# Up-projection of an encoder block: the places of two plain matmuls, of the product copies and of the pair sums are fixed in the instruction order

## The chip, the cores and the metric

The kernel runs on one core of one Trainium2 chip. The metric is the device time of one execution in microseconds (us). The engines are TensorE (PE; its weight loads are a row of their own, PEld), VectorE (DVE), ScalarE (ACT), GpSimd (POOL) and SyncE (SP), which here only issues DMAs.

## The reference

One layer of a streaming encoder on 512 tokens of width 1024: attention, then a gated feed-forward block with a causal convolution of width 3. The change lies in the second part:

```python
def conv_glu(x, w_up, conv_w, conv_b, w_down):
    hid = x @ w_up
    hid = lax.conv_general_dilated(
        hid, conv_w[:, None, :], window_strides=(1,),
        padding=((CONV_WIDTH - 1, 0),),
        dimension_numbers=('NWC', 'WIO', 'NWC'),
        feature_group_count=2 * D_FF) + conv_b
    gate, up = hid[..., :D_FF], hid[..., D_FF:]
    return (jax.nn.silu(gate) * up) @ w_down
...
        x = x + mixed @ w_out[l]
        x = x + conv_glu(rms_norm(x, norm2_g[l]), w_ffn_up[l], ffn_conv_w[l],
                         ffn_conv_b[l], w_ffn_down[l])
```

With D_FF = 2816, the up-projection makes 22 chunks of 128 gate columns and 128 up columns each.

## The kernel before, in words

**Numbers in two halves.** Every operand of a matmul is cut into a high part (a cast to fp32r on ACT) and a low part (the rest, a subtraction on DVE), and each product is three matmuls: high by high, high by low, low by high. `hth` and `htl` are the two halves of the normed activations, transposed, for all 512 tokens; `whi`/`wlo`, `w2h`/`w2l` and `wxh`/`wxl` are halves of weights. The cut of the weights of chunk j + 1 runs while chunk j is multiplied (`run_chunk`, which takes one step of `split_gen` per step of the chunk's body).

**Plain chunks.** Chunks 2, 3, 6, 9, 12, 15, 19 and 21 multiply directly (`up_body`, `up_mm`): 8 steps of the contraction, three matmuls each, for the gate (`pg`) and for the up columns (`pu`), all 512 tokens wide: 48 matmuls. Chunks 0 and 1 do the same in two halves of 256 tokens.

**Seven-product chunks.** The twelve chunks in `SEVEN` (`up_seven`) use seven products of half-size blocks in place of eight. A product is 4 contraction steps by three matmuls, 256 wide, so a chunk is 84 matmuls. There are four banks, `b1`, `b5`, `b7` and `b6`. The first three hold a first product, are copied out to `pc` by ACT (L1177, L1181, L1185), and then a second product is accumulated on top of the first one: the second half of a bank can't begin before its copy. `ts` are sums of token blocks, made once (`token_sums`). From chunk 11 on (`SUMS`) the sums of weight blocks are cut on the chip as well, which adds two casts and two subtractions to the chunk ahead (`split_seven`, L242 and L243).

**Held matmuls.** Where a plain chunk comes ahead of a seven-product one (3, 6, 9, 12, 15 and 19), `up_mm` keeps back the last two matmuls of `pu`: the last three are at L1000, L1001 and L1002, and the latter two are written down behind the first three matmuls of the next chunk's first product (`late["end"]`).

**Behind a chunk.** The gate is convolved and passed through silu (`gate`: ACT L990 and L1014, DVE L992 and L993), so are the up columns, and the two are multiplied (DVE L1089). After every second chunk `pair_sums` makes sums of blocks for the down-projection, which are cut into halves: by DVE (L1053) or, for pairs 1 to 8, by a negated copy on ACT (L1061) and an accumulating DMA of GpSimd (L1062).

**What sets the order.** No one writes the order of an engine by hand. A scheduler places the instructions when the program is built, from the sequence of the source, from priorities (`tc.high_priority`), and from an internal model of when operands are ready. It may therefore put matmuls of a later chunk ahead of matmuls that wait for a copy, and it may take the held matmuls in either order with those of the next chunk. `behind(ins, others)` adds an edge of order alone: the instruction stands after the others, with no semaphore for it.

Of the kernel before, what the change touches and what calls it, by code (L numbers as in the profile page):

```python
# [74 lines left out]
def block_kernel(ctx: ExitStack, tc: tile.TileContext, x, xt, params, g2, rbx, wts, wd0, wd1, out):  # L75
# [28 lines left out]
    G.memset(nhalf, -0.5)  # L104
    qg8 = pool_c.tile([P, 1], F32, tag="qg8", name="qg8")

    def rstd_of(ss, n, width, name):

        r = pool_c.tile([P, 8], F32, tag="rs", name=name, bufs=4)
        V.tensor_scalar(r[:, :n], ss, 1.0 / width, EPS, op0=ALU.mult, op1=ALU.add)  # L110
        G.tensor_tensor(r[:, :n], r[:, :n], nhalf[:, :n], op=ALU.pow)
        return r
# [3 lines left out]
    order = [key for key, _, _ in CHUNKS]  # L116

    pos = {k: i for i, k in enumerate(order)}
    raws, splits, extras, late = {}, {}, {}, {"halves": (), "casts": (), "products": ()}
    FIRST_DN = order.index("dn0_0")  # L120
    keep = {}

# [110 lines left out]
    def split_seven(i, raw, hi, lo):  # L233

        wh, wl = extras.pop(i - pos["up0"])
        splits[order[i]] = tuple(t.rearrange("p (k c) -> p k c", c=P) for t in (hi, lo, wh, wl))
        parts = [(hi, lo, raw, slice(0, 1024)), (hi, lo, raw, slice(1024, 2048))]
        if i - pos["up0"] in SUMS:
            parts[1:1] = [(wh, wl, wl.bitcast(F32), slice(0, 1024))]
            parts += [(wh, wl, wl.bitcast(F32), slice(1024, 1536))]  # L240
        for n, (h, l, src, sl) in enumerate(parts):
            A.copy(h[:, sl], src[:, sl])  # L242
            V.tensor_tensor(l[:, sl], src[:, sl], h[:, sl].bitcast(F32), op=ALU.subtract)  # L243
            if n < len(parts) - 1:
                yield

    def split_gen(i, pieces):

        if i >= len(order):
            return  # L250
        key = order[i]
        kn = CHUNKS[i][1]
        raw = raws.pop(i)
        if is_seven(i) and i - pos["up0"] not in extras:
            fetch_extra(i - pos["up0"])
        sh = 48 if key[:2] in ("qA", "kA", "vB") else 16 if key in ("up0", "up1") or is_seven(i) else 0
        n = 512 * kn if i >= FIRST_DN else 2048
        hi = wp.tile([P, 2112], F32R, tag="whi", name=f"whi_{key}")[:, sh:sh + n]
        lo = wp.tile([P, 2112], F32R, tag="wlo", name=f"wlo_{key}")[:, sh:sh + n]
        splits[key] = (hi.rearrange("p (k c) -> p k c", k=kn), lo.rearrange("p (k c) -> p k c", k=kn))  # L260
        if i >= FIRST_DN:
            yield from split_down(i - FIRST_DN, raw, hi, lo)
        elif is_seven(i):
            yield from split_seven(i, raw, hi, lo)
        n = 2048 // pieces
        cuts = CUTS[0] if i == 0 else [n * j for j in range(pieces + 1)] if i < FIRST_DN and not is_seven(i) else ()
        for j, sl in enumerate(map(slice, cuts, cuts[1:])):
            if i == 0 and j == 0:
                V.tensor_copy(hi[:, sl], raw[:, sl])
            else:  # L270
                A.copy(hi[:, sl], raw[:, sl])  # L271
                if i == 0 and j == 1:
                    yield
                    V.tensor_tensor(lo[:, 0:256], raw[:, 0:256], hi[:, 0:256].bitcast(F32), op=ALU.subtract)
            if (i, j) != (0, 0):
                V.tensor_tensor(lo[:, sl], raw[:, sl], hi[:, sl].bitcast(F32), op=ALU.subtract)  # L276
                if j < len(cuts) - 2:
                    yield


        nxt = {0: None, 1: i + 3, 2: None}.get(i - FIRST_DN, i + 2)
        if nxt is not None and nxt < len(order):
            next(load(nxt))
        j = i + 1 - pos["up0"]
        if j in SEVEN and all(k < j - 2 for k in SEVEN if k < j and (k in SECOND) == (j in SECOND)):
            fetch_extra(j)
        yield
# [433 lines left out]

    a_exps, b_sigs = [], []

    def behind(ins, others):

        for o in others:
            tc.add_manual_dep(ins.ins, o.ins.name, mybir.DependencyInfo(
                mybir.DependencyClass.NoSync, mybir.DependencyReason.DATA), reason="table order")
        return ins

    def soft_b(h, t, ps):


# [261 lines left out]
    def up_mm(ps, hi, lo, o, c0, c1, held=None):  # L995

        for k in range(NK):
            if held is not None and k == NK - 1:
                sh, sl, mh, ml = hi[:, k, o:o + P], lo[:, k, o:o + P], hth[:, k, c0:c1], htl[:, k, c0:c1]
                PE.matmul(ps[:, c0:c1], sh, mh, start=False, stop=False)  # L1000
                held.append(lambda: PE.matmul(ps[:, c0:c1], sh, ml, start=False, stop=False))  # L1001
                held.append(lambda: PE.matmul(ps[:, c0:c1], sl, mh, start=False, stop=True))  # L1002
                yield
# [13 lines left out]
    def pair_sums(i):  # L1017
# [38 lines left out]
        def by_dma():  # L1056

            for a, o, src in ((ay, 256, t["s42"]), (ax, 768, t["st"][:, 0:256]), (ay, 0, u[:, 768:1024]),
                              (ax, 0, u[:, 0:768])):
                n, sl = a.shape[-1] // 2, slice(o, o + src.shape[-1])  # L1060
                A.activation(a[:, n + o:n + sl.stop], src, AF.Copy, scale=-1.0)  # L1061
                G.dma_start(a[:, n + o:n + sl.stop].bitcast(F32), src, accum_op=ALU.add)  # L1062
                A.copy(a[:, sl], src)
        if 0 < i < 9:
# [19 lines left out]
    def up_fin(j, pg, pu, g=None):  # L1084
# [4 lines left out]
        late["fin"] = (V.tensor_tensor(u, g, u, op=ALU.mult),)  # L1089
        if j % 2 == 1 and j // 2 < 9:  # L1090
            steps = pair_sums(j // 2)
            for step in steps:
                step()
            if j // 2 < 7:
                G.dma_start(ayd[j // 2], pairs[j // 2][1].bitcast(F32))

    def up_body(j):
        def body(hi, lo):
# [7 lines left out]

            def end():
                for mm in held or ():
                    mm()
                up_fin(j, pg, pu, g)  # L1110
            if held:
                late["end"] = end
            else:
                end()
            if j in (2, 3):
                next(late["ts"])
        return body
# [39 lines left out]
    def up_seven(j):  # L1157
        def body(hi, lo, wh, wl):
# [6 lines left out]
            def prod(ps, w, b, h, first=True, last=True):  # L1165
                for k in range(4):
                    sh, sl = w[0][:, 4 * b + k, :], w[1][:, 4 * b + k, :]
                    for n, (st, mv) in enumerate(((sh, h[0]), (sh, h[1]), (sl, h[0]))):
                        PE.matmul(ps, st, mv[:, k, :], start=first and k == 0 and n == 0,  # L1169
                                  stop=last and k == 3 and n == 2, skip_group_check=True)  # L1170
                    if late.get("end"):
                        late.pop("end")()
            r, w = (hi, lo), (wh, wl)
            B = lambda a, q: [t[:, 4 * a:4 * a + 4, q] for t in (hth, htl)]
            prod(b1, r, 0, B(0, left), last=False)
            with tc.high_priority(60):
                A.copy(pc[:, 0], b1)  # L1177
            yield
            prod(b5, w, 0, ts[1], last=False)
            with tc.high_priority(60):  # L1180
                A.copy(pc[:, 1], b5)  # L1181
            yield
            prod(b7, r, 1, ts[3], last=False)
            with tc.high_priority(60):
                A.copy(pc[:, 2], b7)  # L1185
            V.tensor_tensor(pc[:, 1], pc[:, 1], pc[:, 2], op=ALU.add)
            yield
            prod(b6, w, 1, ts[2])
            V.tensor_tensor(hu[:, right], b6, pc[:, 0], op=ALU.add)
            yield  # L1190
            prod(b1, r, 2, B(1, left), first=False)
            A.copy(hg[:, left], b1)
            yield
            prod(b5, w, 2, B(1, right), first=False)
            V.tensor_tensor(hg[:, right], b5, hu[:, right], op=ALU.add)
            g = gate(j, hg)
            yield
            prod(b7, r, 3, ts[4], first=False)
            V.tensor_tensor(hu[:, left], b7, hu[:, right], op=ALU.add)
            V.tensor_tensor(hu[:, right], hu[:, right], pc[:, 1], op=ALU.add)  # L1200
            up_fin(j, None, hu, g)
            yield
        return body
# [232 lines left out]
```

## Time and profile before

| | |
|---|---|
| median of 3 runs | 717.42 us (717.33 to 717.8) |
| profiled execution | 718.12 us |
| its span, first to last instruction | 716.4 us |
| TensorE clock granted, mean | 0.999 |
| PE, PEld, DVE, ACT busy in 395 to 607 us | 211.24, 195.71, 180.77, 144.20 us of 212.00 |
| the same in 607 to 716 us | 105.04, 86.23, 90.17, 46.92 us of 109.00 |

The up-projection lies between 395 and 607 us, the down-projection behind it. Matmuls are pipelined: a row's length is that of one matmul from its first read to its modelled end, longer than the distance from one start to the next, and the distance is what counts for throughput. The chain of waits merges neighbours of one line into pieces with a count, so a long piece's length over its count is that distance.

### The profile page before, as it was taken

Reading aid. Unit: us, or ns where it says so; the run is one execution under the profiler, and the core shown is the slowest. Engines: PE = TensorE matmul, PEld = TensorE weight load, DVE = VectorE, ACT = ScalarE, POOL = GpSimd, SP = SyncE. Lnnn points to the kernel's source line nnn. Section 1 sums busy time; section 2 is a strip of 40 time slices with the busy share of each in tenths; the row PEclk is TensorE's granted clock in tenths of the full one; section 3 lists DMA queues with packets and bytes.
Section 4 is the critical chain, followed back from the end, with each engine's and each line's share of the span. In section 5 each row is a group of like instructions: output and inputs, shape, how many; then the busy total and the mean of one; then the engine's idle time right before and its main releaser. Section 6 shows DMA issues by size and latency. Waiting matters only on the chain.

```text
span 716.4 us, 11264 instructions
## 1 busy us (share of the span) xinstructions
PE 709.9 (99%) x4091; PEld 623.6 (87%) x4091; DVE 589.0 (82%) x1049; ACT 432.2 (60%) x803; POOL 85.7 (12%) x123
## 2 busy tenths in 40 slices
PE   9999999999999999999999999999999999999997
PEld 7889998888988888888889889999999998888885
DVE  6668878786999999769475698888788979998686
ACT  6576656667876777434245557668667874544531
POOL 2501200000121211000003002212012111000000
PEclk9999999999999999999999999999999999999999
DMA  9722235444434473685957949999788889674563
GB/s 316 284 82 89 86 121 190 178 162 175 164 130 150 147 280 127 214 305 196 378 198 286 306 172 328 310 359 244 222 213 246 254 232 376 213 245 172 180 206 117
DMA packets 51863, 154.97 MB, mean 216 GB/s; under 512 B 5600, under 2 KB 12384, under 8 KB 44000
## 3 DMA queue, kind: packets, MB, share of 16 engines
q1 hardware_dynamic: 44256, 133.67, 52.9%
q0 software_dynamic: 7264, 20.45, 10.8%
q8 instruction: 32, 0.52, 0.3%
q14 instruction: 23, 0.19, 0.1%
q10 hardware_dynamic: 288, 0.14, 0.1%
HBM read 116.49 MB, written 30.41 MB: 205 GB/s over the span
## 4 chain that ended last, share of the span: by engine, by line
PE 92%; DVE 3%; DMA 3%; SPq 1%; ACT 0%; issue 0%; POOL 0%; DVEq 0%
PE p L1169 16%; PE P L1269 15%; PE vA L433 3%; PE uA L433 3%; PE gB L300 2%; PE gB L301 2%; PE qkB L302 2%; PE gB L302 2%; PE qkB L300 2%; PE qkB L301 2%; PE wo L300 2%; PE wo L301 2%; PE wo L302 2%; PE gA L300 2%; PE pg L300 2%; PE pg L301 2%
## 5 line engine op out<-in xcount | busy, mean ns | idle before, releaser
L165 ACT CAST whi_dn<-raw_dn 128x1024 fp32r<-128x1024 f32 x33 | 34.4, 1052 | 26.5 <-PE P L1269 18.7
L1269 PE MATMUL P<-whi_dn,ax 128*128 128x512 f32 x144 | 44.4, 389 | 0.0
L161 DVE TENSOR_TENSOR wlo_dn<-raw_dn,whi_dn 128x1024 fp32r<-128x1024 f32 x33 | 40.1, 1222 | 5.3 <-ACT whi_dn L165 5.3
L1269 PE MATMUL P<-whi_dn,ay 128*128 128x512 f32 x132 | 40.8, 389 | 0.0
L744 POOL TENSOR_SCALAR_AFFINE_SELECT bB<-bB 128x128 f32<-128x128 f32 x32 | 21.8, 686 | 143.7 <-DVE bB L743 135.1
L1169 PE MATMUL p<-ts,whi_up 128*128 128x256 f32 x192 | 35.5, 279 | 0.0
L301 PE MATMUL pg<-htl,whi_up 128*128 128x512 f32 (+1 forms) x96 | 34.0, 354 | 0.0
L302 PE MATMUL pg<-hth,wlo_up 128*128 128x512 f32 (+1 forms) x96 | 34.0, 354 | 0.0
L300 PE MATMUL pg<-hth,whi_up 128*128 128x512 f32 (+1 forms) x96 | 33.9, 353 | 0.0
L207 DVE TENSOR_TENSOR pkr<-pkr 128x512 f32<-128x512 f32 x40 | 27.4, 686 | 7.0 <-DMA pkr<-in_wts 4.1
L1269 PEld LDWEIGHTS P<-whi_dn,ax 128*128 128x128 f32 x144 | 27.0, 188 | 5.6
L301 PE MATMUL pu<-htl,whi_up 128*128 128x512 f32 (+1 forms) x90 | 31.5, 351 | 0.0
L300 PE MATMUL pu<-hth,whi_up 128*128 128x512 f32 (+1 forms) x90 | 31.5, 350 | 0.0
L302 PE MATMUL pu<-hth,wlo_up 128*128 128x512 f32 (+1 forms) x90 | 31.5, 349 | 0.0
L243 DVE TENSOR_TENSOR wlo_up<-raw_up,whi_up 128x1024 fp32r<-128x1024 f32 x24 | 28.8, 1219 | 1.7 <-ACT whi_up L242 1.7
L1169 PEld LDWEIGHTS p<-ts,whi_up 128*128 128x128 f32 x192 | 29.6, 189 | 0.1
L1269 PEld LDWEIGHTS P<-whi_dn,ay 128*128 128x128 f32 x132 | 24.8, 188 | 5.1
L1269 PE MATMUL P<-wlo_dn,ax 128*128 128x512 f32 x72 | 28.0, 389 | 0.0
L742 DVE TENSOR_TENSOR_SCAN aB<-aB,reset 128x127 f32<-128x127 f32 (+3 forms) x32 | 25.9, 816 | 2.6 <-ACT aB L737 2.5
L1169 PE MATMUL p<-ts,wlo_up 128*128 128x256 f32 x96 | 26.9, 280 | 0.8 <-DVE wlo_up L243 0.8
L276 DVE TENSOR_TENSOR wlo_up<-raw_up,whi_up 128x1024 fp32r<-128x1024 f32 (+1 forms) x26 | 24.6, 973 | 2.9 <-ACT whi_up L271 2.8
L1169 PE MATMUL p<-hth,whi_up 128*128 128x256 f32 x96 | 26.8, 279 | 0.0
(350 smaller groups left out, 2539.2 us busy)
## 6 DMA issues: line engine op xcount, KB each, us to landing
parked<-pkr SPq DMA_DIRECT2D x45, 256.0 KB, 2.8
raw_dn<-in_wd SPq DMA_DIRECT2D x11, 1024.0 KB, 4.9
pkr<-in_wts SPq DMA_DIRECT2D x10, 1024.0 KB, 6.8
raw_up<-in_wts SPq DMA_DIRECT2D x10, 1024.0 KB, 5.3
raw_up<-in_wts SPq DMA_DIRECT2D x12, 512.0 KB, 6.1
raw_dn<-in_wd SPq DMA_DIRECT2D x11, 512.0 KB, 3.5
wxl_up<-parked SPq DMA_DIRECT2D x21, 256.0 KB, 5.7
ayd<-ay POOLq DMA_DIRECT2D x7, 768.0 KB, 6.8
```

The lines of the kernel that those rows point to most:

```text
L161: chain("halves", V.tensor_tensor(o, x, y, op=op))
L165: chain("casts", A.copy(hi[:, sl], src))
L207: V.tensor_tensor(b[o], b[x], b[y], op=op)
L243: V.tensor_tensor(l[:, sl], src[:, sl], h[:, sl].bitcast(F32), op=ALU.subtract)
L276: V.tensor_tensor(lo[:, sl], raw[:, sl], hi[:, sl].bitcast(F32), op=ALU.subtract)
L300: ins = PE.matmul(ps, sh, mh, start=first, stop=False)
L301: PE.matmul(ps, sh, ml, start=False, stop=False)
L302: PE.matmul(ps, sl, mh, start=False, stop=last)
L433: PE.matmul(pss[t], st[:, 4 * half + k, t * P:(t + 1) * P], mv[:, k, :], start=half == 0 and k == 0 and j == 0, stop=half == 1 and k == 3 ...
L742: V.tensor_tensor_scan(ar, ar, reset[:, S - n:S - 1][:, ::-1], 1.0, op0=ALU.mult, op1=ALU.max)
L1169: PE.matmul(ps, st, mv[:, k, :], start=first and k == 0 and n == 0, stop=last and k == 3 and n == 2, skip_group_check=True)
L1269: chain("products", PE.matmul(dst, st, mv, start=first and n == 0, stop=last and n == 2, skip_group_check=True))
```

## The change

Five edits, all in the up-projection; the amount of arithmetic is the same.

1. *The held pair.* The last matmul of a plain chunk that is not kept back (`late["pre"]`) stands ahead of the next chunk's first three, these ahead of the two held ones, and every further matmul of seven-product chunks is put behind the last of the pair (`late["flip"]`). Each edge is of order alone.
2. *The casts of weights.* Each cast of `split_seven` and `split_gen` is put behind the copy of a product that was written last (`late["pcs"]`), so the casts of the next chunk's later parts follow the copies of `b1`, `b5` and `b7`.
3. *The pair sums.* Only the first step stays in `up_fin`; the rest is kept in `owed` and paid in a later chunk, after the third copy (with the negated copies behind it, `late["copied"]`) or at the end of chunk 2, 6 or 12. Pair 8 is paid at once.
4. *The sums of `hu`.* The left half takes the fourth product and the right half is derived from it; four additions as before.
5. `behind` stands further up in the file.

```diff
         for n, (h, l, src, sl) in enumerate(parts):
-            A.copy(h[:, sl], src[:, sl])
+            behind(A.copy(h[:, sl], src[:, sl]), late["pcs"])
...
-                A.copy(hi[:, sl], raw[:, sl])
+                behind(A.copy(hi[:, sl], raw[:, sl]), late["pcs"])
...
-                PE.matmul(ps[:, c0:c1], sh, mh, start=False, stop=False)
+                late["pre"] = (PE.matmul(ps[:, c0:c1], sh, mh, start=False, stop=False),)
...
-                A.activation(a[:, n + o:n + sl.stop], src, AF.Copy, scale=-1.0)
+                behind(A.activation(a[:, n + o:n + sl.stop], src, AF.Copy, scale=-1.0), late["copied"])
...
             steps = pair_sums(j // 2)
-            for step in steps:
-                step()
-            if j // 2 < 7:
-                G.dma_start(ayd[j // 2], pairs[j // 2][1].bitcast(F32))
+            steps[0]()
+
+            def rest_(i=j // 2):
+                for step in steps[1:]:
+                    step()
+                if i < 7:
+                    G.dma_start(ayd[i], pairs[i][1].bitcast(F32))
+            owed.append(rest_)
+            if j == 17:
+                owed.pop()()
...
                 for mm in held or ():
-                    mm()
+                    late["flip"] = (behind(mm(), late["flip"]),)
                 up_fin(j, pg, pu, g)
...
+            if j % 2 == 0:
+                pay()
...
-                        PE.matmul(ps, st, mv[:, k, :], start=first and k == 0 and n == 0,
-                                  stop=last and k == 3 and n == 2, skip_group_check=True)
+                        mm = PE.matmul(ps, st, mv[:, k, :], start=first and k == 0 and n == 0,
+                                       stop=last and k == 3 and n == 2, skip_group_check=True)
+                        behind(mm, late["pre" if late.get("end") else "flip"])
                     if late.get("end"):
+                        late["flip"] = (mm,)
                         late.pop("end")()
...
             with tc.high_priority(60):
-                A.copy(pc[:, 0], b1)
+                late["pcs"] = (A.copy(pc[:, 0], b1),)
...
+            if j % 2 == (j - j % 2 in SEVEN and j - j % 2 + 1 in SEVEN):
+                late["copied"] = (third,)
+                pay()
             prod(b6, w, 1, ts[2])
-            V.tensor_tensor(hu[:, right], b6, pc[:, 0], op=ALU.add)
+            V.tensor_tensor(hu[:, left], b6, pc[:, 0], op=ALU.add)
+            V.tensor_tensor(hu[:, right], hu[:, left], pc[:, 1], op=ALU.add)
...
-            V.tensor_tensor(hg[:, right], b5, hu[:, right], op=ALU.add)
+            V.tensor_tensor(hg[:, right], b5, hu[:, left], op=ALU.add)
...
-            V.tensor_tensor(hu[:, left], b7, hu[:, right], op=ALU.add)
-            V.tensor_tensor(hu[:, right], hu[:, right], pc[:, 1], op=ALU.add)
+            V.tensor_tensor(hu[:, left], b7, hu[:, left], op=ALU.add)
```

The order of PE where plain chunk 12 gives way to chunk 13, before. `pu12` is the bank of the up columns of chunk 12, `p1_13` and `p5_13` are the banks `b1` and `b5` of chunk 13:

```order
L302 MATMUL pu12_5571<-hth_102,wlo_up12_5447 128x512
L1000 MATMUL pu12_5571<-hth_102,whi_up12_5446 128x512
L1001 MATMUL pu12_5571<-htl_103,whi_up12_5446 128x512
L1002 MATMUL pu12_5571<-hth_102,wlo_up12_5447 128x512
L1169 MATMUL p5_13_5641<-ts1_4467,wxh_up13_5469 128x256 x2
L1169 MATMUL p1_13_5640<-hth_102,whi_up13_5584 128x256
L1169 MATMUL p1_13_5640<-htl_103,whi_up13_5584 128x256
L1169 MATMUL p5_13_5641<-ts1_4467,wxl_up13_5470 128x256
```

The same place now:

```order
L309 MATMUL pu12_5558<-hth_102,wlo_up12_5434 128x512
L1000 MATMUL pu12_5558<-hth_102,whi_up12_5433 128x512
L1185 MATMUL p1_13_5640<-hth_102,whi_up13_5571 128x256
L1185 MATMUL p1_13_5640<-htl_103,whi_up13_5571 128x256
L1185 MATMUL p1_13_5640<-hth_102,wlo_up13_5572 128x256
L1001 MATMUL pu12_5558<-htl_103,whi_up12_5433 128x512
L1002 MATMUL pu12_5558<-hth_102,wlo_up12_5434 128x512
```

Three 256-wide matmuls of the first product now stand between L1000 and the two held ones. Before, this was so ahead of chunks 4, 7 and 10; now it is ahead of 4, 7, 10, 13, 16 and 20.

The order of ACT while chunk 4 is multiplied, before. `ub` and `cg` belong to the convolutions of chunks 2 and 3, `ax0` and `ay0` to the sums of pair 0, `pc4` are the copies of the products of chunk 4:

```order
L1052 CAST ax0_4402<-ub_4147 128x768
L242 CAST whi_up5_4622<-raw_up5_4450 128x1024 x2
L990 ACTIVATE ub_4147<-pu3_4502,par_91 128x512
L1014 ACTIVATE cg2_4462<-cg2_4462 128x512
L1177 COPY pc4_4580<-p1_4_4576 128x256
L1052 CAST ay0_4403<-st0_4404 128x512
L1181 COPY pc4_4580<-p5_4_4577 128x256
L1185 COPY pc4_4580<-p7_4_4578 128x256
L990 ACTIVATE cg3_4543<-pg3_4501,par_91 128x512
```

And now:

```order
L1052 CAST ax0_4402<-ub_4147 128x768
L990 ACTIVATE ub_4147<-pu3_4502,par_91 128x512
L1014 ACTIVATE cg2_4453<-cg2_4453 128x512
L1195 COPY pc4_4580<-p1_4_4576 128x256
L1052 CAST ay0_4403<-st0_4404 128x512
L249 CAST whi_up5_4609<-raw_up5_4441 128x1024
L1199 COPY pc4_4580<-p5_4_4577 128x256
L249 CAST whi_up5_4609<-raw_up5_4441 128x1024
L990 ACTIVATE cg3_4543<-pg3_4501,par_91 128x512
L1203 COPY pc4_4580<-p7_4_4578 128x256
```

The two casts of the next chunk's weights went from ahead of all three copies to behind the first and behind the second.

The order of PE at the end of chunk 14, now; `pg15` is the gate bank of plain chunk 15, `p7_14` is `b7` of chunk 14:

```order
L1185 MATMUL p5_14_5777<-hth_102,w2l_up14_5623 128x256
L307 MATMUL pg15_5913<-hth_102,whi_up15_5796 128x512
L1185 MATMUL p7_14_5778<-ts4_4573,whi_up14_5666 128x256 x2
L1185 MATMUL p7_14_5778<-ts4_4573,wlo_up14_5667 128x256
L308 MATMUL pg15_5913<-htl_103,whi_up15_5796 128x512
```

Single plain matmuls can still stand between products at the end of a chunk (between the last two rows stand the other nine of `p7_14`). Such short runs of plain matmuls stand in chunk 5 (three, then five; 12 matmuls of the chunk behind each), 11 (two; 12), 14 (one; 12) and 18 (one; 24).

More of the change, by code (lines that the diff above doesn't have):

```diff
@@ L105, in block_kernel, with behind @@
     qg8 = pool_c.tile([P, 1], F32, tag="qg8", name="qg8")
+    def behind(ins, others):
+        for o in others:
+            tc.add_manual_dep(ins.ins, o.ins.name, mybir.DependencyInfo(
+                mybir.DependencyClass.NoSync, mybir.DependencyReason.DATA), reason="table order")
+        return ins
     def rstd_of(ss, n, width, name):
@@ L118, in block_kernel @@
     pos = {k: i for i, k in enumerate(order)}
-    raws, splits, extras, late = {}, {}, {}, {"halves": (), "casts": (), "products": ()}
+    raws, splits, extras, late = {}, {}, {}, {"halves": (), "casts": (), "products": (), "pcs": ()}
     FIRST_DN = order.index("dn0_0")
@@ L722, in block_kernel @@
     a_exps, b_sigs = [], []
[L724 to L729, printed above, removed]
     def soft_b(h, t, ps):
@@ L1091, in up_fin, with pay @@
             steps = pair_sums(j // 2)
-            for step in steps:
-                step()
-            if j // 2 < 7:
-                G.dma_start(ayd[j // 2], pairs[j // 2][1].bitcast(F32))
+            steps[0]()
[7 more added lines that the diff above has]
+                owed.pop()()
+    owed = []
+    late["copied"] = ()
+    def pay():
+        if owed:
+            owed.pop()()
     def up_body(j):
@@ L1180, in body @@
             with tc.high_priority(60):
-                A.copy(pc[:, 1], b5)
+                late["pcs"] = (A.copy(pc[:, 1], b5),)
             yield
@@ L1184, in body @@
             with tc.high_priority(60):
-                A.copy(pc[:, 2], b7)
+                third = A.copy(pc[:, 2], b7)
+            late["pcs"] = (third,)
             V.tensor_tensor(pc[:, 1], pc[:, 1], pc[:, 2], op=ALU.add)
             yield
+            if j % 2 == (j - j % 2 in SEVEN and j - j % 2 + 1 in SEVEN):
+                late["copied"] = (third,)
+                pay()
             prod(b6, w, 1, ts[2])
-            V.tensor_tensor(hu[:, right], b6, pc[:, 0], op=ALU.add)
+            V.tensor_tensor(hu[:, left], b6, pc[:, 0], op=ALU.add)
+            V.tensor_tensor(hu[:, right], hu[:, left], pc[:, 1], op=ALU.add)
             yield
```

## The prediction

> **What bounds the kernel now.** I read the page first, then the waits of TensorE (PE), then the chain of waits in order of time, then the timeline of PE around single places. The page's span, its first row and the row of the granted clock:
>
> ```profile
> span 716.4 us, 11264 instructions
> PE 709.9 (99%) x4091; PEld 623.6 (87%) x4091; DVE 589.0 (82%) x1049; ACT 432.2 (60%) x803; POOL 85.7 (12%) x123
> PEclk9999999999999999999999999999999999999999
> ```
>
> PE is never free and its clock is granted in full. So an edit can gain in two ways only: by removing one of PE's few waits, or by making PE's own instructions follow each other faster. All waits of PE that the profile has (engine, line, released by: us in total, times, longest):
>
> ```profile
> PE warm L352 <- DVE warm L349: 1.1, 1, 1.1
> PE p L1169 <- DVE wlo_up L243: 0.8, 1, 0.8
> PE gA L300 <- DVE mixA L622: 0.3, 1, 0.3
> ```
>
> Only the second lies in the part that the change touches. A busy PE need not be a fast one, though. The chain that ended last runs through PE for the whole up-projection, and its pieces are long stretches of one line with their counts (start, length, line, count); L1169 are the 256-wide matmuls of the seven-product chunks, L1269 the 512-wide ones of the down-projection:
>
> ```profile
> 443.41 4.24 PE p L1169 x36
> 455.07 14.51 PE p L1169 x128
> 470.51 2.83 PE p L1169 x24
> 474.04 1.36 PE p L1169 x12
> 485.09 14.63 PE p L1169 x129
> 505.63 4.24 PE p L1169 x36
> 514.88 15.55 PE p L1169 x132
> 536.35 4.24 PE p L1169 x36
> 545.61 25.44 PE p L1169 x216
> 576.28 4.24 PE p L1169 x36
> 586.22 9.89 PE p L1169 x84
> 607.02 105.03 PE P L1269 x462
> ```
>
> Divide length by count. 14.51/128 and 14.63/129 are 113.4 ns; 15.55/132 and 25.44/216 are 117.8 ns; 4.24/36, 2.83/24 and 9.89/84 are 117.7 to 117.9. The same instruction runs at one of two cadences, 4.4 ns apart, and keeps its cadence through 216 instructions on end, while the work on the other engines changes all the time. At 512 wide it is 105.03/462 = 227.3 ns, twice the fast one. What distinguishes the stretches is how they begin. The timeline of PE just ahead of the fast 128 (start, length, line, names, form):
>
> ```profile
> 453.86 0.39 PE L1000 MATMUL pu<-hth,whi_up 128*128 128x512 f32 x1
> 454.09 0.28 PE L1169 MATMUL p<-hth,whi_up 128*128 128x256 f32 x1
> 454.21 0.28 PE L1169 MATMUL p<-htl,whi_up 128*128 128x256 f32 x1
> 454.33 0.28 PE L1169 MATMUL p<-hth,wlo_up 128*128 128x256 f32 x1
> 454.44 0.40 PE L1001 MATMUL pu<-htl,whi_up 128*128 128x512 f32 x1
> 454.68 0.40 PE L1002 MATMUL pu<-hth,wlo_up 128*128 128x512 f32 x1
> 454.91 0.28 PE L1169 MATMUL p<-hth,whi_up 128*128 128x256 f32 x1
> 455.03 0.28 PE L1169 MATMUL p<-htl,whi_up 128*128 128x256 f32 x1
> 455.14 0.28 PE L1169 MATMUL p<-hth,wlo_up 128*128 128x256 f32 x1
> ```
>
> Starts tell the cadence: three 256-wide ones 0.12 apart (454.09 to 454.44 is 0.35, 117 ns each), two plain 512-wide ones, and from 455.03 on 0.113. Behind a long run of plain matmuls, then, 256-wide ones begin slow and stay slow; "three, two plain, the rest" turns them fast. In the old order this pattern stands only ahead of chunks 4, 7 and 10, the three that begin fast. Ahead of 13, 16 and 20 the two plain ones stand before the three, and there everything up to the next plain run is slow (514.88, 545.61, 586.22).
>
> **The change part by part.** *The tie on PE.* The new order has the pattern ahead of all six of these chunks, and the early pieces of the plain chunks 6, 9, 12, 15, 19 no longer cut 36 at 117.8 off the end of the seven-product chunk ahead. Matmuls are neither added nor removed. At 117.8 ns stand in the old order: 36 + 24 + 36 + 132 + 36 + 216 + 36 + 84 = 600. In the new order all of them follow a pattern, except 72 that come right behind a short run of plain ones: 12 behind three, 12 behind five (both up 5), 12 behind two (up 11), 12 behind one (up 14), 24 behind one (up 18). The chain has short runs with both outcomes (the 24 at 470.51 slow, the 12 at 474.04 fast), so these 72 are bounded by 0 and 72 x 4.4 ns = 0.32 us. I take those behind two or three as fast, since two turn the state in the rows above, and the other 48 as slow. Gain: 552 x 4.4 ns = 2.43 us, with ends 528 (2.32) and 600 (2.64). All of it is on the path that sets the end, since PE waits nowhere from 430 us on. Three more sets of three now run slow ahead of their pair of plain ones: 9 x 4.4 ns = 0.04 lost. The first plain ones behind 256-wide ones are some ns late too (454.44 to 454.91 is 0.47 for two, against 0.455), but there are about as many such switches after as before; I put 0 with 0.1 either way.
>
> *The copies on ScalarE (ACT).* Their price shows where the wait of 0.8 us lies, in chunk 4. PE, VectorE (DVE) and ACT there, in the timeline:
>
> ```profile
> 424.54 0.39 PE L1169 MATMUL p<-ts,wxh_up 128*128 128x256 f32 x2
> 428.62 0.39 PE L1169 MATMUL p<-ts,whi_up 128*128 128x256 f32 x2
> 429.89 0.39 PE L1169 MATMUL p<-ts,wlo_up 128*128 128x256 f32 x1 [0.76 <-DVE wlo_up L243]
> ...
> 428.61 2.35 DVE L243 TENSOR_TENSOR wlo_up<-raw_up,whi_up 128x1024 fp32r<-128x1024 f32 x2
> 430.88 0.74 DVE L992 SCALAR_TENSOR_TENSOR ub<-pu,par,ub 128x511 f32<-128x511 f32 x1
> ...
> 426.94 1.99 ACT L242 CAST whi_up<-raw_up 128x1024 fp32r<-128x1024 f32 x2
> 428.84 0.77 ACT L990 ACTIVATE ub<-pu,par 128x512 f32<-128x512 f32 x1
> 429.51 0.62 ACT L1014 ACTIVATE cg<-cg 128x512 f32<-128x512 f32 x1
> 430.03 0.35 ACT L1177 COPY pc<-p 128x256 f32<-128x256 f32 x1
> 430.28 0.62 ACT L1052 CAST ay<-st 128x512 fp32r<-128x512 f32 x1
> 432.26 0.78 ACT L990 ACTIVATE cg<-pg,par 128x512 f32<-128x512 f32 x1 [0.81 <-DVE ub L1089]
> ```
>
> PE finished the four first halves of chunk 4 at 428.62. The second half of each product accumulates into the same bank and so waits for its copy, and the first copy is only at 430.03. So the old order goes to chunk 5 instead, and its fourth matmul, on a low half of the weights, waits until 429.89: three steps of 0.113 would have had it at 428.96, so 0.93 us are lost, and with some slow steps behind it about 1.04. In the new order both casts of whi_up5 stand behind copies. ACT's rows overlap by 0.1 us, so I take each 0.1 shorter. From 426.94: ub 0.67, cg 0.52, copy 0.25: the first copy has landed by 428.5, and PE goes on into the second half at 428.62 without a wait. Then ay 0.52, half a cast 0.95, the second copy: landed at 430.2, while PE wants it at 428.62 + 12 x 0.113 = 429.98. Then half a cast 0.95, cg 0.68, the third copy: 432.1, wanted at 430.23 + 1.36 = 431.6. Waits of about 0.3 and 0.5, in sum 0.8, take the place of 1.04: gain 0.24. The low half that PE waited for is now cut by DVE behind four rows of about 0.65 (the one at 430.88 is the first), so at 428.61 + 2.6 + 1.2 = 432.4; PE asks for it after 432.1 + 1.36 + 0.34 = 433.8. The first sum hu, which frees the bank that chunk 5's first product takes, follows both low halves on DVE: 428.61 + 2.6 + 2.3 + 0.3 = 433.8, the same moment, so nearly late as well. What is late next is the third copy. Bounds: the wait is gone (gain 1.04), or a copy comes 1 us later than I reckon (loss 1). The casts of the later chunks move behind copies as well; there they are hidden as long as a copy lands within 36 x 0.113 = 4.1 us of its product.
>
> *The pair sums paid later, the queues, the other order of hu.* These are the same instructions at other places, and PE reads none of the pair sums before the down-projection: 0. If that cover went, one DVE step of 0.4 to 1.2 us would show, which the third rival takes up. On SP's queue a store of ax1 moves behind six loads, and the reload of ax0 ahead of the weights of chunk 20. Loads of that kind land like this (KB each, median us to landing):
>
> ```profile
> raw_up<-in_wts SPq DMA_DIRECT2D x12, 512.0 KB, 6.1
> ```
>
> They are issued about a chunk of 84 x 0.113 = 9.5 us ahead of their casts, so 3 us of shift are hidden: 0, and up to 1 us lost if chunk 20's weights come later than that. GpSimd only changes the order of a few accumulating DMAs, for which PE doesn't wait.
>
> Sum: 2.43 - 0.04 + 0.24 = 2.6 us. The profiled execution took 718.12, its span is 716.4, and the median of the runs is 717.42; the gain is in PE's stream and so the same for each: 715.5, 713.8 and **714.8**. Only over 0.2% (1.43 us) can be told from no change here.
>
> **The rivals.** *The cadence is not set by the order.* The slow stretches may be slow for a reason that belongs to the late chunks (their weights are cut on the chip from chunk 11 on), and the pattern ahead of the fast three may be chance. For it: every chunk from 13 on is slow throughout. Against it: the fast 129 at 485.09 hold chunk 11's first products, and the slow 36 and 24 at 443.41 and 470.51 are chunks 5 and 8, which are not cut so. It leaves the copies alone: 717.42 - 0.24 = 717.2. Chance 0.08. The Trainium skill, "TensorE: Matmul & The Clock Gate", section "Wait — 56ns, not 53.3ns?", speaks for this rival: a warm matmul follows the last after its columns divided by 2.4 GHz plus a fixed 2.5 ns, which is 109 ns at 256 columns whatever stood before, and by that rule alone the sum would be 0 for the tie. The two cadences of the chain, 113.4 and 117.8 ns for one form, do not agree with it.
>
> *ACT falls behind its own copies.* ACT works in order, and now every cast for the next chunk stands between copies that wait for PE. At chunk 4 the first copy came 5.5 us behind its product (424.54 to 430.03). Were ACT as far in arrears at each of the six places where one seven-product chunk follows another (4, 7, 10, 13, 16, 17), each would cost PE the 0.8 us of chunk 4: 717.42 - 2.39 - 1.04 + 6 x 0.8 = 718.8, which is where slower by over 0.2% begins; at 1.2 each it gives 721.2. So it decides from 0.8 us each. Against it stands ACT's load behind chunk 4 (columns: window, length, busy time of PE, PEld, DVE, ACT, POOL):
>
> ```profile
> 454.00:607.00 153.00, 153.00 (x1084) 143.30 (x1083) 129.77 (x204) 108.76 (x186) 29.40 (x38) 1.00 0.90 274
> ```
>
> 108.76 of 153 is 71%, which leaves time to catch up in every plain chunk. Chance of slower 0.07.
>
> *DVE becomes the bound at the handover.* It is busy 129.77 of 153 us, 85%, so if PE comes to the down-projection 2.4 us sooner, the low halves of its weights may not be there. PE would give back up to those 2.4: 717.2 at worst, 716 at half. DVE's amount of work is unchanged and 15% of 153 is 23 us, so I give it 0.08.
>
> **How the numbers follow.** Forecast 0.77, cadence 0.08, ACT slower 0.07, DVE 0.08. The forecast's own ends: 2.64 + 0.1 + 1.04 = 3.8 gives 713.6; 2.32 - 0.04 - 0.1 - 1.0 = 1.2 gives 716.2. The range 713.6 to 716.8 holds the forecast and most of the DVE case, and leaves out the cadence rival, the slower ACT case and the worst of DVE's. Faster by over 0.2%, below 715.98: 0.77 less a little for its upper end, plus the mild half of DVE's: 0.77. Within: 0.16. Slower: 0.07.
>
> **What would show it.** Right: the chain of waits after has 256-wide pieces of 150 to 220 matmuls at 113.4 ns each, and no long one at 117.8; in chunk 4 PE waits for copies of ACT and no more for wlo_up; nothing else waits between 430 and 607 us. Wrong in the main term: the pattern stands in the timeline and the pieces behind it still divide to 117.8. Wrong through ACT: waits "PE p <- ACT pc" at chunks 7, 10, 13, 16, 17. Wrong through DVE: a wait "PE P <- DVE wlo_dn" in the down-projection.

## The result and the profile after

| | before | changed |
|---|---|---|
| median of 15 runs on the same chips | 717.58 us | 715.65 us (714.17 to 717.0) |
| profiled execution, its span | 718.12, 716.4 us | 717.0, 715.3 us |

The ratio to the kernel before is 0.9971, with a 95% interval of 0.9963 to 0.9979, so 2.1 us are won, 1.5 to 2.7. The forecast was 714.8 and the range 713.6 to 716.8. The profiled execution of the changed kernel, 717.0 us, is the slowest of its 15, so its waits show a late execution and not the usual one.

The page of the changed kernel begins with these rows:

```profile
span 715.3 us, 11278 instructions
PE 708.5 (99%) x4091; PEld 622.1 (87%) x4091; DVE 588.7 (82%) x1049; ACT 431.7 (60%) x803; POOL 85.9 (12%) x123
```

Busy shares tell nothing here, as before. The chain of waits does (start, length, line, count; L1185 are now the 256-wide matmuls):

```profile
486.36 17.35 PE p L1185 x153
504.18 1.37 PE p L1185 x12
...
516.36 17.35 PE p L1185 x153
533.94 1.38 PE p L1185 x12
...
546.36 25.51 PE p L1185 x225
572.10 2.73 PE p L1185 x24
585.06 0.35 PE p L1185 x3
585.88 9.19 PE p L1185 x81
```

17.35/153, 25.51/225 and 9.19/81 are 113.4 ns: chunks 10 to 20 keep the quick cadence to their end. Of the longer pieces none is slow; sets of three such as the one at 585.06 remain at 117 ns. The waits of PE (engine, line, released by: us in total, times, longest) show what came in exchange:

```profile
PE p L1185 <- ACT pc L1195: 0.7, 2, 0.5
...
PE p L1185 <- ACT pc L1203: 0.2, 1, 0.2
```

The wait for `wlo_up` is gone, and PE waits for three copies. Two are in chunk 4, where the forecast has them; the longest is in chunk 7, where it has none ("nothing else waits between 430 and 607 us"). The timeline of ACT there, and PE's row:

```profile
457.28 0.42 ACT L1061 ACTIVATE ax<-st 128x256 fp32r<-128x256 f32 x1 [2.01 <-DVE st L1044]
457.60 0.40 ACT L1063 CAST ax<-st 128x256 fp32r<-128x256 f32 x1
457.90 0.84 ACT L1061 ACTIVATE ax<-ub 128x768 fp32r<-128x768 f32 x1
458.65 0.82 ACT L1063 CAST ax<-ub 128x768 fp32r<-128x768 f32 x1
459.37 0.63 ACT L1061 ACTIVATE ay<-st 128x512 fp32r<-128x512 f32 x1
459.90 0.60 ACT L1063 CAST ay<-st 128x512 fp32r<-128x512 f32 x1
460.41 0.77 ACT L990 ACTIVATE ub<-pu,par 128x512 f32<-128x512 f32 x1
461.08 0.62 ACT L1014 ACTIVATE cg<-cg 128x512 f32<-128x512 f32 x1
461.61 0.35 ACT L1195 COPY pc<-p 128x256 f32<-128x256 f32 x1
...
462.01 0.38 PE L1185 MATMUL p<-hth,whi_up 128*128 128x256 f32 x1 [0.54 <-ACT pc L1195]
```

The first copy of chunk 7 stands behind six rows for the sums of pair 2, a tap and a silu. ACT idled for 2.0 us until DVE had the sum `st`, and began on them only at 457.28.

**The difference, term by term.** Distances between the starts of neighbouring matmuls give each part. In the traces of the two kernels, 616 and 36 of the 256-wide matmuls follow at 116 to 120 ns: 580 x 4.4 ns = 2.55 us won (the sets of three are in both counts). Steps longer than that add up to 1.03 us in chunk 4 before and 1.31 after (0.28 lost), and to 0.81 in chunk 7 (lost). PE came to chunk 4 at 423.18 and not 422.70 (0.48 lost ahead of the change). The down-projection has 0.07 less. Sum 1.05, and the spans differ by 1.1.

A second trace of the changed kernel (715.71 us, close to the median; span 714.0; below) has 30 at the slow cadence (2.58 won), nothing lost in chunk 4 (1.03 won), 1.10 lost in chunk 7, 0.25 lost ahead and 0.07 won: 2.33, and its span is 2.4 shorter. So the cadence term is the same in both traces, chunk 7 roughly, and chunk 4 is not.

### The profile page after: what moved, and what is told of

It reads as the page before. It is cut to its first block, busy times and chain, and to the rows that moved or that the text cites. A ratio compares the mean times of both kernels' runs of the same rounds, so it can differ in the third digit from the quotient of the medians.

```text
span 715.3 us, 11278 instructions
## 1 busy us (share of the span) xinstructions
PE 708.5 (99%) x4091; PEld 622.1 (87%) x4091; DVE 588.7 (82%) x1049; ACT 431.7 (60%) x803; POOL 85.9 (12%) x123
## 4 chain that ended last, share of the span: by engine, by line
PE 87%; DVE 5%; DMA 2%; ACT 2%; issue 1%; SPq 1%; POOL 0%; DVEq 0%; ACTq 0%
PE P L1291 15%; PE p L1185 12%; PE vA L440 3%; PE uA L440 3%; PE gB L307 2%; PE qkB L309 2%; PE gB L308 2%; PE gB L309 2%; PE qkB L307 2%; PE qkB L308 2%; PE wo L308 2%; PE wo L309 2%; PE wo L307 2%; PE gA L307 2%; PE gA L308 2%; PE gA L309 2%
## 5 line engine op out<-in xcount | busy, mean ns | idle before, releaser
L1185 PE MATMUL p<-ts,whi_up 128*128 128x256 f32 x192 | 34.1, 277 | 0.2 <-ACT pc L1203 0.2
L1185 PEld LDWEIGHTS p<-ts,whi_up 128*128 128x128 f32 x192 | 29.2, 188 | 0.7 <-ACT pc L1203 0.4
L1185 PE MATMUL p<-hth,whi_up 128*128 128x256 f32 x96 | 26.8, 279 | 0.7 <-ACT pc L1195 0.7
L1185 PE MATMUL p<-hth,wlo_up 128*128 128x256 f32 x96 | 26.5, 276 | 0.0
```

The lines of the kernel that those rows point to most:

```text
L1185: mm = PE.matmul(ps, st, mv[:, k, :], start=first and k == 0 and n == 0, stop=last and k == 3 and n == 2, skip_group_check=True)
```

## The experiments

The theory going in: the order of PE sets the cadence, and the waits come from copies standing behind other rows on ACT. The rivals: the cadence belongs to the late chunks, the tie on PE is needed as such, and the waits belong to the order alone and not to when data land.

**Edit 1 alone, on the kernel before.**

```diff
-                PE.matmul(ps[:, c0:c1], sh, mh, start=False, stop=False)
+                late["pre"] = (PE.matmul(ps[:, c0:c1], sh, mh, start=False, stop=False),)
...
-                    mm()
+                    late["flip"] = (behind(mm(), late["flip"]),)
...
+                        behind(mm, late["pre" if late.get("end") else "flip"])
...
+                        late["flip"] = (mm,)
```

> The kernel before with edit 1 alone: the pattern (three 256-wide, two plain, the rest) is tied ahead of all six chunks, while the casts, copies and pair sums are as before. Theory (the order of PE sets the cadence): the pieces behind the patterns run at 113.4 ns; only the 36, 12, 24, 12, 24, 36, 24 and some 3 matmuls behind the short or long plain runs at the ends of chunks 5, 8, 11, 14 and 18 stay at 117.8, 171 in place of 600, so 429 x 4.4 ns = 1.9 us are won; the wait of about 1.0 us in chunk 4 stays. 715.7 us beside 717.6 for the kernel before. Rival (the late chunks are slow for another reason, the gain came from the copies): 717.6, and the pieces of chunks 13, 16 and 20 still divide to 117.8 ns.

Measured: 715.78 us, ratio 0.9971 (0.9961 to 0.9981). Its chain from chunk 10 on:

```profile
515.40 14.63 PE p L1169 x129
533.00 4.24 PE p L1169 x36
544.75 0.35 PE p L1169 x3
545.57 24.15 PE p L1169 x213
570.64 2.83 PE p L1169 x24
```

14.63/129 and 24.15/213 are 113.4: chunks 13 and 16 to 18, at 117.8 throughout before, are quick behind the pattern and slow again behind plain matmuls (the 36 and the 24). 276 are left at the slow cadence, against 171 expected: the sets of three (18) were not in that count, and some 80 stand behind a wait of 0.1 us in chunk 4, from which PE came out at 118 ns. That wait was expected at 1.0 us, and one of 0.83 for the first copy of chunk 10 was new. The cadence term holds in kind but is smaller, (616 - 276) x 4.4 ns = 1.5 us in place of 1.9; the waits came out otherwise. That the time still met the 715.7 forecast is partly luck.

**All but edit 1.** The changed kernel without the ties on PE.

```diff
-                late["pre"] = (PE.matmul(ps[:, c0:c1], sh, mh, start=False, stop=False),)
+                PE.matmul(ps[:, c0:c1], sh, mh, start=False, stop=False)
...
-                    late["flip"] = (behind(mm(), late["flip"]),)
+                    mm()
...
-                        behind(mm, late["pre" if late.get("end") else "flip"])
...
-                        late["flip"] = (mm,)
```

> The changed kernel with edit 1 taken out: copies, pair sums and the sums of hu as in the change, PE not tied. In the order of its instructions the pattern stands ahead of all six chunks all the same, since the casts no longer come early. Theory (only the order that PE ends up with counts): as the changed kernel, 715.65, with its waits of 1.3 us in chunk 4 and 0.8 us in chunk 7 and the cadence of 113.4 ns from chunk 13 on. Rival (the tie itself is needed, by some effect of its edges): the late chunks at 117.8 ns, some 2 us more, 717.6.

Measured: 715.4 us, ratio 0.9967 (0.9956 to 0.9979). Its chain has the pieces of the changed kernel:

```profile
484.90 17.35 PE p L1185 x153
514.90 17.35 PE p L1185 x153
544.90 25.51 PE p L1185 x225
```

The tie on PE isn't needed once the rows on ACT are placed: the scheduler then keeps the pattern by itself. Each half of the change brings about all of its gain, since either puts the pattern ahead of all six chunks. Chunk 7 lost 0.79 us, as expected; chunk 4 lost nothing, which the theory did not expect.

**The sums of pair 2 behind the third copy of chunk 7.**

```diff
-                A.copy(a[:, sl], src)
+                behind(A.copy(a[:, sl], src), late["copied"])
...
-            if j % 2 == 0:
+            if j in (2, 12):
                 pay()
...
-            if j % 2 == (j - j % 2 in SEVEN and j - j % 2 + 1 in SEVEN):
+            if j == 7 or j % 2 == (j - j % 2 in SEVEN and j - j % 2 + 1 in SEVEN):
```

> The changed kernel with the sums of pair 2 paid in chunk 7 behind its third copy, not at the end of chunk 6, and with all casts of paid sums behind that copy too. Theory (the wait of 0.8 us in chunk 7 is the first copy standing behind six rows of pair 2 on ACT): that wait goes, chunk 4 keeps its 1.3 us, 715.65 - 0.8 = 714.8. Rival (ACT is late there by the rows of chunk 6 itself, the taps and the silu, or the rows moved behind the third copy make a later copy late): the wait stays or comes back in chunk 8, 715.65.

Measured: 715.02 us (714.12 to 715.26), ratio 0.9958 (0.9945 to 0.9971). The waits of PE in the up-projection are gone altogether; what is new:

```profile
PE P L1291 <- DVE wlo_dn L168: 0.3, 1, 0.3
```

The wait in chunk 7 was the rows of pair 2: shown, since all four traces of kernels that pay them at the end of chunk 6 lost 0.74 to 1.10 us there, and this one none. The steps around the new wait, at 609 us, add up to 0.53 us. It carries the third rival's sign: the low half of the down-projection's weights is not ready. In the changed kernel it was 0. That PE's earlier arrival is the cause is not shown; more on it below.

**The first copy ahead of the tails of the plain chunks.** On top of the last one, taps and product of the plain chunk, and in chunk 4 the sums of pair 0, are written behind the first copy.

```diff
-                up_fin(j, pg, pu, g)
+                if held:
+                    late["tail"] = lambda: up_fin(j, pg, pu, g)
+                else:
+                    up_fin(j, pg, pu, g)
...
                 late["pcs"] = (A.copy(pc[:, 0], b1),)
+            if late.get("tail"):
+                if j == 4:
+                    late["copied"] = late["pcs"]
+                    pay()
+                late.pop("tail")()
...
```

> As the run with pair 2 paid later, and in each of the six chunks the tail of the plain chunk ahead (its taps, its product) is written behind the first copy; pair 0 is paid in chunk 4 behind the first copy as well. Theory (ACT lateness of the first copies is the whole of the waits): the first copy of chunk 4 lands by 425.6 and is no longer waited for; the second stands behind four casts of pair 0 (1.9 us), a tap (0.67), half a cast (0.95) and a tap (0.68), at 429.8, and is wanted at 430.0; so of 1.3 us at most 0.3 stay: 715.65 - 0.8 - 1.0 = 713.9. Rival (DVE becomes the bound in chunk 4: its low halves or the taps of the plain chunk come later and a bank or wlo_up is waited for): PE waits for DVE by about what is saved, 714.8.

Measured: 714.77 us (714.06 to 715.83), ratio 0.9957 (0.9945 to 0.9969). No wait in chunks 4 and 7, and 0.11 us at the down-projection. The first copy of chunk 4 started at 425.83, the second at 430.24, and nobody waited. Against the kernel above the gain can't be told from none; the 1.3 us of chunk 4 were not there to be saved in that one either.

**The pair turned round.** The kernel with pair 2 paid later, and the two plain matmuls ahead of the three everywhere.

```diff
-                    if late.get("end"):
-                        late["flip"] = (mm,)
-                        late.pop("end")()
...
+            if late.get("end"):
+                late["flip"] = late["pre"]
+                late.pop("end")()
             prod(b1, r, 0, B(0, left), last=False)
```

> The run with pair 2 paid later (715.0), with one thing turned round: in all six places the two plain matmuls stand ahead of the three 256-wide ones, so that all plain matmuls of a chunk are behind each other and the pattern stands nowhere. Theory (the order sets the cadence): all pieces behind the plain chunks run at 117.8 ns, 168 + 168 + 168 + 144 + 228 + 84 = 960 matmuls x 4.4 ns = 4.2 us more, 719.2; the 24 behind three plain ones in chunks 14 and 18 are open. Rival (the cadence belongs to something else than the order of the pair): 715.0.

Measured: 718.16 us, ratio 1.001 (1.0001 to 1.0019), so slower than the kernel before by a hair.

```profile
423.07 19.79 PE p L1185 x168
453.76 19.79 PE p L1185 x168
...
515.15 16.96 PE p L1185 x144
532.81 2.72 PE p L1185 x24
545.75 26.86 PE p L1185 x228
```

19.79/168, 16.96/144 and 26.86/228 are 117.8 ns, chunk 4 included; the 24 behind three plain ones run at 113.4. This settles the first rival: the same chunks on the same data go at either cadence by where two matmuls stand. It cost 3.1 us by the medians; but the two kernels ran on different chips, and by their ratios to the kernel before, each beside its own runs, it is 0.0052 of 717, or 3.7. Expected were 4.2. From the last transpose to the last 256-wide matmul it is 4.0 us longer (207.8 against 203.8), but PE began 0.4 earlier in this trace, and 0.8 came back behind, 0.45 of it in a down-projection that no longer waits for its weights.

**How many plain ones, how many ahead.** Two single executions, each with six settings of the pattern in the kernel with pair 2 paid later.

```diff
+HELD = {4: 1, 7: 3, 10: 4, 13: 5, 16: 6, 20: 8}
...
-            yield from up_mm(pu, hi, lo, P, 0, S, held)
+            yield from up_mm(pu, hi, lo, P, 0, S, held, HELD.get(j + 1, 2))
```

> One look. The kernel with pair 2 paid later, with a different number of plain matmuls between the three and the rest in each place: 1 at chunk 4, 3 at 7, 4 at 10, 5 at 13, 6 at 16, 8 at 20 (2 before). Theory (a short run of plain matmuls turns the state only for some lengths, as after fast ones in the traces so far, where 1, 2, 3 and 5 leave it fast and 4, 7 and 12 or more make it slow): 1, 3 and 5 give 113.4 ns, 4, 6 and 8 give 117.8 ns. Rival (any plain matmul behind three 256-wide ones turns it): all six pieces at 113.4 ns.

Measured: 718.27 us (span 716.5). The chain (L1004 are the held plain ones) behind 4, 5, 6 and 8:

```profile
484.48 0.93 PE pu L1004 x4
485.41 19.43 PE p L1193 x165
...
514.97 1.16 PE pu L1004 x5
516.13 17.36 PE p L1193 x153
...
544.77 1.39 PE pu L1004 x6
546.16 26.50 PE p L1193 x225
...
584.87 1.84 PE pu L1004 x8
586.71 9.54 PE p L1193 x81
```

Behind 4, 6 and 8 it is 117.8 ns, behind 5 it is 113.5; behind 1 and 3 the starts in chunks 4 and 7 are 113.4 apart. The theory's list holds, and the rival (any plain matmul turns it) falls. Each count stood at one place here, but counted over all 14 traces four plain ones stand in nine places and six, seven and eight in two each, always slow behind; five stand in six places, always quick. Not all of this trace is free of waits: chunk 4 lost 0.86 us and chunk 7 0.52, where ACT's copy stood behind a silu that waited for DVE. So moving pair 2 does not shield chunk 7 from a late DVE.

```diff
+AHEAD = {4: 1, 7: 2, 10: 4, 13: 6, 16: 9, 20: 12}
...
-                    if late.get("end"):
+                        if late.get("end") and 3 * k + n + 1 == AHEAD.get(j, 3):
```

> One look. The same kernel with two plain matmuls in each place and another number of 256-wide ones ahead of them: 1 at chunk 4, 2 at 7, 4 at 10, 6 at 13, 9 at 16, 12 at 20. Theory (two plain ones turn the state whatever the number of slow ones ahead, since the slow state repeats itself from the first matmul on): all six pieces at 113.4 ns. Rival (the three matter as three, one step of the contraction): only 6, 9 and 12, or none, at 113.4.

Measured: 714.66 us. The chain behind 1, 2, 4, 6, 9 and 12 ahead:

```profile
423.90 18.95 PE p L1193 x167
454.01 18.82 PE p L1193 x166
484.22 18.59 PE p L1193 x164
514.44 17.01 PE p L1193 x150
544.81 24.83 PE p L1193 x219
...
584.82 8.17 PE p L1193 x72
```

All six are at 113.4 to 113.5. How many stand ahead is of no matter; one is enough to cut the pair off the long stretch. What decides, as long as PE does not wait, is the length of the last unbroken stretch of plain matmuls, whatever the cadence ahead of it was.

**The changed kernel once more.**

> One more look at the changed kernel itself. Theory (the 1.3 us of waits in chunk 4 hang on when the transposed activations xT land for DVE, 20.5 us behind the first matmul of the up-projection in the first look, and vary from execution to execution; the 0.8 us in chunk 7 belong to the order): chunk 7 waits for its first copy by 0.7 to 0.9 again, and the waits of chunk 4 are 1.3 us only if DVE starts as late, near 0 if it starts 1 us sooner. Rival (both belong to the order): 1.3 and 0.8 again.

Measured: 715.71 us. Its waits have chunk 7 alone:

```profile
PE p L1185 <- ACT pc L1195: 0.8, 1, 0.8
```

DVE's first row on `xT` and ACT's first copy of chunk 4, in the first trace and then in the second:

```profile
406.54 1.23 DVE L1158 TENSOR_TENSOR xT<-xT 128x1024 f32<-128x1024 f32 x1 [4.87 <-DMA xT<-htd]
...
429.03 0.36 ACT L1195 COPY pc<-p 128x256 f32<-128x256 f32 x1
```

```profile
404.61 1.23 DVE L1158 TENSOR_TENSOR xT<-xT 128x1024 f32<-128x1024 f32 x1 [3.17 <-DMA xT<-htd]
...
427.11 0.36 ACT L1195 COPY pc<-p 128x256 f32<-128x256 f32 x1
```

DVE waits for the same DMA in both. It starts 1.93 us sooner in the second, and the copy, 22.5 us behind, comes 1.92 us sooner: DVE's queue passes the delay on undiminished, ACT waits for DVE's sums, and PE for ACT. The traces of five other kernels whose ACT has the same order in chunk 4 bear it out: the copy comes 22.5 us behind the `xT` row in each, and DVE is never idle in between. That is the 1.3 us.

**The landing of xT made late.** Four DMAs that nothing reads ahead of the loads of `xT`, in the changed kernel and in the one with the first copy ahead.

```diff
+        for t in range(2):
+            for b in range(2):
+                SP.dma_start(pad[t, b].rearrange("p (k q) -> p k q", k=4)[:, :, 0:P],
+                             htd[t, b].rearrange("p (k q) -> p k q", k=4)[:, :, 0:P])
```

> One look. The changed kernel with four more DMAs, which nothing reads, ahead of the loads of xT on SP's queue, so that the transposed activations come later by about 4 x 0.62 us (what one issue took on that queue); ACT's cast of ay0 from st0 also comes to stand ahead of the first copy of chunk 4. Theory (the waits of chunk 4 hang on when xT lands): DVE's first row on xT starts 18 us or more behind the last transpose, and chunk 4 waits 1.3 us or more, beside none in the second look at the changed kernel, where it started 16.4 us behind; some 717. Rival (the waits in the first look were an accident of something else): no waits in chunk 4, 715.7.

> One look. The kernel with the tails of the plain chunks written behind the first copies, with the same four DMAs ahead of the loads of xT. Theory (its first copy no longer stands behind rows that wait for DVE): with DVE as late as in the run with the changed kernel, chunk 4 waits at most 0.5 us in sum, some 715.2. Rival (a later copy, or a low half, waits for DVE all the same): 1 us or more in chunk 4.

Measured: 715.86 and 715.5 us. The edit did not do what it was meant to. SP issued the four DMAs already at 380 to 385 us, and the loads of `xT` only from 394.3 and 394.7 (393.4 to 394.2 in the other traces), so they delayed little. In the first, DVE began on `xT` at 405.69, between the two traces without the DMAs, 17.0 us ahead of chunk 4's first product (16.6 and 18.3 there), and chunk 4 lost 0.39 us. That fits the theory's direction, but it is one more sample and no test; the condition of the expectation, 18 us or more behind the last transpose, did not arise (17.4). In the second, `xT` was not late (404.98), so the remedy was not put to its test. But chunk 4 lost 0.26 us for the second copy at a lead of 18.3 us, at which the changed kernel lost none.

**The kernel before once more.**

> One more look at the kernel before. Theory (its wait of 1.0 us in chunk 4, too, hangs on the landing of xT, where DVE started 17.7 us behind the last transpose in the first look): if DVE starts 17 us behind or sooner, PE waits 0.1 us or less for wlo_up of chunk 5; the pieces at 117.8 ns are the same as in the first look, 600 and a few. Rival (the wait belongs to the old order): about 1.0 us again whatever DVE's start.

Measured: 719.01 us. DVE was as late as in the first trace (17.3 us behind the last transpose in both) and the wait nearly the same, 1.02 us; the condition of the expectation did not arise. What can be said comes from edit 1 alone, where ACT has the old order in chunk 4: DVE began 16.4 us behind the last transpose, and 0.10 us were lost. The other half of the expectation, the same pieces at 117.8 ns, failed: 748 matmuls follow at the slow cadence, not 616. The pieces of chunks 4 and 7:

```profile
429.52 9.81 PE p L1169 x81
...
455.04 14.94 PE p L1169 x128
```

The first trace has 9.48 and 14.51 us for them. In chunk 4 the 80 matmuls behind the wait ran at 118 ns, and at 113 before. In chunk 7, 79 ran at 118 behind a single step of 186 ns, 0.07 us too long, which the table of waits does not list. So one order can run at different cadences; 132 more matmuls at the slow one are 0.6 us.

**No short stretches.** The kernel with the first copy ahead, and the first gate and up matmul of each plain chunk tied behind the last products of the chunk ahead.

```diff
+        if late.pop("first", False):
+            behind(ins, late.get("flip", ()))
...
+            late["flip"] = late["mm"]
```

> The kernel with the tails of the plain chunks behind the first copies, and the first gate and up matmul of each plain chunk tied behind the last products of the chunk ahead, so that no short run of plain matmuls is left. Theory: all 256-wide matmuls but the three ahead of each pair run at 113.4 ns; that is 48 fewer at 117.8 than without the tie, 0.2 us, and three interruptions of 20 ns less: 714.77 - 0.25 = 714.5, if no product at the end of chunks 5 and 18 waits for its copy. Rival (the early plain matmuls covered a wait for a copy, or the down-projection's weights are late by as much): 714.8 or more, with a wait in chunk 5 or 18 or for wlo_dn behind 608 us.

Measured: 715.93 us (714.15 to 718.71), ratio 0.9978 (0.9963 to 0.9993). All 256-wide pieces but the sets of three, and 12 matmuls between two short waits in chunk 20, are at 113.4, as meant. But in the profiled execution, at 718.25 us one of the three slowest of ten, PE waits:

```profile
PE p L1192 <- ACT pc L1212: 1.8, 1, 1.8
...
PE P L1305 <- DVE wlo_dn L168: 0.7, 1, 0.7
```

`xT` was late here (DVE's row at 405.60, and at 404.02 in the kernel it is made from), and now the second copy of chunk 4 stood behind ACT's rows for pair 0, until 431.82. So putting the first copy ahead moves the exposure to a late `xT` to the second copy. Chunk 4 lost 2.03 us in all, chunk 20 another 0.59 in short waits for copies, and the handover to the down-projection 1.29. The rival's time and its wait for `wlo_dn` came, though the copies waited for are in chunks 4 and 20, not in 5 or 18. That the tie is to blame is not shown: `xT` was late in this execution, and the interval overlaps with that of the kernel it is made from (0.9945 to 0.9969). Of the versions tried, the one with pair 2 paid later (715.02) is the simplest that is ahead of the changed kernel, but their intervals overlap.

## Why the prediction was right, and where not

*The cadence.* Right in kind and size: 2.39 us forecast with the sets of three, 2.55 and 2.58 measured. The first rival and the rule beside it fall. The Trainium skill, "TensorE: Matmul & The Clock Gate", section "Wait — 56ns, not 53.3ns?", has one distance for a width, by its formula an estimated 109 ns at 256 columns. No row here shows it: the shortest step behind a 256-wide matmul in the trace before is 112 ns, and the measured 113.4 and 117.8 ns decide. One step of the reasoning was too narrow: the pattern needs no three. The 48 matmuls put down as slow, 36 behind single plain ones and 12 behind five, were at 113 ns after three steps.

*The copies in chunk 4.* The step "waits of about 0.3 and 0.5, in sum 0.8, take the place of 1.04" failed. It takes the lateness of one execution for the kernel's. The first trace after has 1.31, the second none. The lead of DVE's first `xT` row over chunk 4's first product tells them apart. In the old order of ACT it is 17.1 us in both traces before (1.0 lost in each) and 18.0 in edit 1 alone (0.10). In the new one it is 16.6 (1.31 lost), 17.3 in the trace with six counts held (0.86), and 18.2 and more in five traces (0). The size does not follow from the lead alone: at 17.0 the trace with the added DMAs lost only 0.39; there the cast of `ay0` stands ahead of the first copy, and the second copy comes 0.6 us sooner behind the `xT` row than in the changed kernel. What makes `xT` late stays open: the two traces of the changed kernel issue the first of its loads only 0.2 us apart (394.24 and 394.01), and DVE starts 12.3 and 10.6 us behind that.

*The pair sums paid later.* "These are the same instructions at other places, and PE reads none of the pair sums before the down-projection: 0" is the step that failed most clearly. Readers on PE were asked for, and not who stands behind these rows on ACT: the first copy of chunk 7. It cost 0.81 and 1.10 us in the two traces and 0.79 without edit 1, and went when the rows were moved. This is the second rival's mechanism at one of its six places, at just the 0.8 us from which it was to decide; at one place it can't.

*The rest.* Switches and queues at 0 show as that. The third rival did not come in the changed kernel. Its wait takes 0.5 and 0.1 us in the kernel with pair 2 paid later and the one made from it, whose last products come at 592.2 us, where the changed kernel's come at 594.8 and 593.5. But an early PE does not explain it alone: the kernel without short stretches lost 1.3 us there with its last products at 595.0, where DVE itself waited 1.7 us for the load of the weights, and the second trace of the kernel before lost 0.3 with them at 596.5.

*Luck.* In the second trace, which is close to the median, the two misses nearly cancel: chunk 4 gave 1.03 us where 0.24 was forecast, and chunk 7 took 1.10 where 0 was. The cadence term was right by its reasoning; that the sum of 2.6 came so near to the 2.1 measured was in part luck.

## What to carry to other kernels

A busy engine may hold two paces for one instruction: divide the chain's long pieces by their counts, compare how the pieces begin, and turn the order round in one experiment. A row that is moved costs what stands behind it on its engine, even where nobody reads its result. A wait in one profiled execution is a sample: follow it back to its first cause, and if that is a DMA, take a second trace before pricing what replaces it. A delay put in on purpose must be checked in the trace: here the added DMAs ran long before the load that they were to delay.

## What the runs showed of the hardware

A long row of 256-wide matmuls runs at 113.4 or 117.8 ns each, and which is set by the number of 512-wide ones in the unbroken stretch ahead: 1, 2, 3 or 5 give 113.4 (in some places only after three steps of 114 to 125), 4, 6, 7, 8 and every stretch of 12 or more give 117.8. In the up-projections of the 14 traces no stretch of a seven-product chunk begins otherwise; 9 to 11 do not occur. The quick cadence held for up to 249 matmuls on end, the slow one for up to 228. A wait can set it anew: of two waits of 1.0 us at the same place, one left 113 and the other 118 ns behind it. Single steps of 135, 154, 186 and 210 ns, 0.02 to 0.10 us too long, each left 118. Why, no run here shows.
